# Index scores of a sparse-attention step: the high x low products on 64 rows, two heads at once

## The chip, the cores and the metric

The kernel runs on one core of a Trainium2 chip. The metric is the device time of one execution in microseconds (us); a kernel's time is the median of its runs.

## The reference

One step of a decoder layer that runs sparse attention and retention side by side, for 1024 prompt tokens and 8 sequences of 4 new tokens each. What matters here is the indexer of the sparse attention: for each query it scores every key with four small heads, and the 256 best keys are kept.

```
def index_scores(qi, wi, ki):                      # 4 heads of 64, float32
    s = jnp.einsum('bqhd,bsd->bqhs', qi, ki)
    w = wi * (N_HEADS_IDX ** -0.5 * HEAD_DIM_IDX ** -0.5)
    return jnp.einsum('bqhs,bqh->bqs', jax.nn.relu(s), w)

def select_keys(scores, q_pos, topk):
    admissible = jnp.arange(S)[None, None, :] <= q_pos[None, :, None]
    _, idx = lax.top_k(jnp.where(admissible, scores, -jnp.inf), topk)
```

Everything is float32, and the choice of keys hangs on small differences, so the scores need float32's precision.

## The kernel before, in words

**Precision.** A float32 number x is held as two FP32R numbers, high = x rounded and low = x - high, and a product is summed over high and low parts. For the projections (`terms`, lines 209 to 211) that is three products: high x high, high x low, low x high.

**Index scores.** A head has 64 numbers, half of TensorE's 128 rows. So `use_qi` (line 665) puts the query's high part into rows 0 to 63 of the tile `QS[h]` and its low part into rows 64 to 127. To do so it copies the projection's output to both halves on ACT (lines 675 and 676) and then subtracts on DVE, in place, for the low part (line 677). It is called for two heads at a time (`h0` = 0 or 2), and for two pieces of 400 tokens (`late`). `use_ki` (line 680) writes the key's high part to both halves of `KH` and its low part to both halves of `KL`. One 128-row product of `QS[h]` with `KH` is then high x high + low x high, and one with `KL` is high x low + low x low.

**The score loop** (line 705) goes over the query blocks b = 7 down to 2 of 128 tokens, each with W = 128 (b + 1) keys, and over the four heads. A head gets a buffer `pl()` in PSUM: 1024 columns, two such buffers in all. For each chunk of up to 512 keys there is a product with `KH` (line 712) and one with `KL` (line 713) into the same place. Then ACT takes the relu into `rl` (line 715, two buffers), and DVE multiplies by the head's weight and adds to `SC[b]` (lines 717 and 719).

**The order.** The program text isn't the order in which an engine issues. The kernel is built with `schedule_with_timeline_sim=True`: a planner walks the instructions with times of its own and writes down an order for each engine, and the chip keeps that order. `issue_after` puts instructions behind a given one. The helper `together` (line 169) uses it for groups of small products on parts of the array; the score loop doesn't use it. What stands in the text behind the score loop is free to run among it: the projections of the gates and of the retention (lines 209 to 211, into the two `pj` buffers), and the gather and transposes of the cached index keys for the new tokens (lines 751 to 767).

**Behind it.** The scores feed the search for the 256th largest (`pick_all`, lines 795 to 873: 32 rounds of counting, on DVE for blocks 6 to 2, on ACT for block 7 and the new tokens). The search shares the time with the retention's projections and small products; line 556 is its 64-row score product, one head on each half of the array.

Of the kernel before, what the change touches and what calls it, by code (L numbers as in the profile page):

```python
# [8 lines left out]
F32 = mybir.dt.float32  # L9
# [3 lines left out]
AF = mybir.ActivationFunctionType  # L13
OP = mybir.AluOpType
# [13 lines left out]
LK = PAST + NS  # L28
# [83 lines left out]
def hybrid_step(tc, A, outs, dbg=None):  # L112
    ctx = ExitStack()
    with ctx:
        _hybrid_step(ctx, tc, A, outs, dbg or {})


def _hybrid_step(ctx, tc, A, outs, dbg):
    nc = tc.nc
    f32 = lambda ap: ap.bitcast(F32)  # L120
# [17 lines left out]
    def pl():  # L138
        return ps.tile([128, 1024], F32, name="pl", bufs=2)

    def pt():
        return ps.tile([128, 512], F32, name="pt", bufs=2)
# [89 lines left out]
    with ExitStack() as s0:  # L232
# [127 lines left out]
        W, ws = [], []  # L360
# [288 lines left out]
    with ExitStack() as s1:  # L649
        scp = s1.enter_context(tc.tile_pool(name="scp", bufs=1, reuse_waits="tile"))  # L650
        SC = {b: scp.tile([128, (b + 1) * 128], F32, name=f"sc{b}") for b in range(2, 8)}
        SCS = scp.tile([NS, LK], F32, name="scs")
        gp = s1.enter_context(tc.tile_pool(name="gp", bufs=1, reuse_waits="tile"))
        with ExitStack() as s2:
            ip = s2.enter_context(tc.tile_pool(name="ip", bufs=1, reuse_waits="tile"))
            QS = [ip.tile([128, TT], F32R, name=f"qs{h}") for h in range(4)]
            KH = ip.tile([128, TT], F32R, name="kih")
            KL = ip.tile([128, TT], F32R, name="kil")
# [4 lines left out]
            wsc = ip.tile([128, 9, 4], F32, name="wsc")  # L663

            def use_qi(h0):
                def use(c, p):
                    sl = late[c]
                    for i in (0, 1):
                        src, q = p[64 * i:64 * i + 64], QS[h0 + i]
                        if c == 1:  # L670
                            h = 4 * (h0 + i)
                            for o in (0, 64):
                                nc.vector.tensor_copy(QF[o:o + 64, :, h:h + 4],
                                                      src[:, T - sl.start:].rearrange("p (b i) -> p b i", b=NB))
                        nc.scalar.copy(q[0:64, sl], src)
                        nc.scalar.copy(q[64:128, sl], src)
                        nc.vector.tensor_sub(q[64:128, sl], src, f32(q[64:128, sl]))
                return use

            def use_ki(c, p):  # L680
# [9 lines left out]
            for g in range(3):  # L690
                p = pt().rearrange("p (t c) -> p t c", c=128)
# [12 lines left out]

            for b in range(7, 1, -1):
                W = (b + 1) * 128
                for h in range(4):
                    p = pl()
                    for n0 in range(0, W, 512):
                        n1 = min(W, n0 + 512)  # L710
                        q = QS[h][:, b * 128:b * 128 + 128]
                        nc.tensor.matmul(p[:, n0:n1], q, KH[:, n0:n1], start=True, stop=False)
                        nc.tensor.matmul(p[:, n0:n1], q, KL[:, n0:n1], start=False, stop=True)
                    rl = ip.tile([128, LK], F32, name="rl", bufs=2)
                    nc.scalar.activation(rl[:, :W], p[:, :W], AF.Relu)
                    if h == 0:
                        nc.vector.tensor_scalar(SC[b], rl[:, :W], wsc[:, b, 0:1], None, op0=OP.mult)
                    else:
                        nc.vector.scalar_tensor_tensor(SC[b], rl[:, :W], wsc[:, b, h:h + 1], SC[b], op0=OP.mult, op1=OP.add)
                nc.vector.tensor_add(SC[b][:, W - 128:W], SC[b][:, W - 128:W], C[:, C_CAUS:C_CAUS + 128])  # L720


# [16 lines left out]
            for G in (0, 1):  # L739
                p = pt()[:, :128]  # L740
# [6 lines left out]
            for G in (0, 1):  # L747
                KP = []
                for b in range(4 * G, 4 * G + 4):
# [5 lines left out]
                    p = pt()  # L755
# [6 lines left out]
                for o in (0, 64):  # L762
                    for b4 in range(4):
                        nc.tensor.matmul(x[32 * b4:32 * b4 + 32, 8 * o:8 * o + 512], QF[o:o + 64, 4 * G + b4], KP[b4][o:o + 64],
                                         start=True, stop=True)
                for b4 in range(4):
                    nc.tensor.matmul(xn[32 * b4:32 * b4 + 32, :NS], QF[0:64, 4 * G + b4], kiT[0:64, T:], start=True, stop=True)
                rl = ip.tile([128, LK], F32, name="rl", bufs=2)
# [620 lines left out]
```

## Time and profile before

| | |
|---|---|
| median of 3 runs | 1141.44 us (1141.26 to 1142.6) |
| profiled execution | 1139.63 us, its span 1137.8 us |
| TensorE (PE) busy | 1089.7 us, 96% of the span |
| DVE busy | 679.5 us, 60% |
| ACT busy | 471.1 us, 41% |
| granted TensorE clock | 0.995 of full speed |

In the rows of the profile a line such as L712 is a line of the kernel; PE is TensorE's products, PEld its weight loads. A group row gives the engine, the operation, the tiles written and read, the tile shape with rows x columns of the array, the count, the busy time with the mean duration in ns, and the idle time before it with what ended it. A timeline row gives the start and the length in us. Durations of products overlap, because they are pipelined: what one costs is the step to the next start. A few product records are missing in the trace.

### The profile page before, as it was taken

Reading aid. Unit: us, or ns where it says so; the run is one execution under the profiler, and the core shown is the slowest. Engines: PE = TensorE matmul, PEld = TensorE weight load, DVE = VectorE, ACT = ScalarE, POOL = GpSimd, SP = SyncE. Lnnn points to the kernel's source line nnn. Section 1 sums busy time; section 2 is a strip of 40 time slices with the busy share of each in tenths; the row PEclk is TensorE's granted clock in tenths of the full one; section 3 lists DMA queues with packets and bytes.
Section 4 is the critical chain, followed back from the end, with each engine's and each line's share of the span. In section 5 each row is a group of like instructions: output and inputs, shape, how many; then the busy total and the mean of one; then the engine's idle time right before and its main releaser. Section 6 shows DMA issues by size and latency. Waiting matters only on the chain.

```text
span 1137.8 us, 20198 instructions
## 1 busy us (share of the span) xinstructions
PE 1089.7 (96%) x7978; PEld 986.6 (87%) x7978; DVE 679.5 (60%) x1637; ACT 471.1 (41%) x910; POOL 226.2 (20%) x194
## 2 busy tenths in 40 slices
PE   6989999999989999999999999999989999999997
PEld 5779788899879999999989999777989888898886
DVE  6775369999999865943223122101357767588645
ACT  6574355654565332232233322211336666443111
POOL 0012015023310311012332212143013333100000
PEclk9999999999999999999999999999999999999999
DMA  9933334135233524422876676596899741483321
GB/s 311 229 89 94 101 113 133 41 108 153 80 91 108 151 77 131 130 61 78 275 253 211 218 222 175 187 312 225 278 267 256 197 111 31 156 269 118 116 93 56
DMA packets 157237, 179.32 MB, mean 158 GB/s; under 512 B 18821, under 2 KB 129101, under 8 KB 156054
## 3 DMA queue, kind: packets, MB, share of 16 engines
q1 hardware_dynamic: 147208, 142.31, 42.4%
q0 software_dynamic: 9856, 35.66, 9.7%
q8 instruction: 63, 1.03, 0.4%
q14 instruction: 32, 0.26, 0.1%
q10 hardware_dynamic: 78, 0.06, 0.0%
HBM read 137.23 MB, written 36.98 MB: 153 GB/s over the span
## 4 chain that ended last, share of the span: by engine, by line
PE 74%; DVE 12%; DMA 5%; ACT 4%; issue 3%; SPq 1%; DVEq 0%; ACTq 0%
PE pj L209 13%; PE pj L211 13%; PE pj L210 13%; DVE eq L795 4%; PE po L1173 3%; PE pj L1327 3%; PE pj L1326 3%; PE pj L1325 3%; PE str L1014 2%; PE tr L1156 2%; PE pj L949 2%; PE pj L950 2%; PE pj L951 2%; ACT ra L802 2%; PE sx L1042 1%
## 5 line engine op out<-in xcount | busy, mean ns | idle before, releaser
L209 PE MATMUL pj<-hh,wh 128*128 128x352 f32 (+1 forms) x1168 | 384.5, 329 | 10.8 <-ACT qs L451 4.4
L211 PE MATMUL pj<-hh,wl 128*128 128x352 f32 (+1 forms) x1168 | 378.8, 324 | 0.0
L210 PE MATMUL pj<-hl,wh 128*128 128x352 f32 (+1 forms) x1168 | 378.2, 324 | 0.0
L209 PEld LDWEIGHTS pj<-hh,wh 128*128 128x128 f32 x1168 | 220.1, 188 | 20.7 <-issue 8.1
L211 PEld LDWEIGHTS pj<-hh,wl 128*128 128x128 f32 x1168 | 219.9, 188 | 4.8 <-issue 4.1
L210 PEld LDWEIGHTS pj<-hl,wh 128*128 128x128 f32 x1168 | 220.8, 189 | 2.9 <-issue 2.5
L795 DVE TENSOR_SCALAR_CACHE_REDUCE eq<-sc,cand 128x896 bf16<-128x896 f32 (+4 forms) x155 | 135.6, 875 | 2.4
L195 ACT CAST wh<-ws 128x1024 fp32r<-128x1024 f32 (+1 forms) x65 | 61.1, 941 | 115.6 <-PE pj L210 67.7
L196 DVE TENSOR_TENSOR wl<-ws,wh 128x1024 fp32r<-128x1024 f32 (+1 forms) x48 | 51.8, 1082 | 59.3 <-ACT wh L195 59.2
L196 POOL TENSOR_TENSOR wl<-ws,wh 128x1024 fp32r<-128x1024 f32 x17 | 41.4, 2437 | 166.9 <-ACT wh L195 166.7
L1143 POOL TENSOR_SCALAR lg<-lg,st 128x1024 f32<-128x1024 f32 (+7 forms) x64 | 48.2, 759 | 121.6 <-DVE st L1142 73.2
L802 ACT ACTIVATE ra<-sc,cand 128x1024 bf16<-128x1024 f32 x31 | 35.7, 1151 | 59.7 <-DVE cand L873 58.7
L1141 ACT ACTIVATE lg<-lg,st 128x1024 f32<-128x1024 f32 (+7 forms) x64 | 49.5, 775 | 24.7 <-DVE st L1140 22.5
L1016 DVE COPY kt<-str 128x512 f32<-128x512 f32 x32 | 22.1, 690 | 61.2 <-PE str L1014 57.6
L643 ACT ACTIVATE raw<-pj 128x352 f32<-128x352 f32 x48 | 22.2, 462 | 77.7 <-PE pj L211 74.5
L1325 PE MATMUL pj<-woh,MH 128*128 128x512 f32 (+1 forms) x136 | 51.3, 377 | 0.0
L1326 PE MATMUL pj<-wol,MH 128*128 128x512 f32 (+1 forms) x136 | 51.2, 377 | 0.0
L1327 PE MATMUL pj<-woh,ML 128*128 128x512 f32 (+1 forms) x136 | 51.2, 377 | 0.0
L984 POOL DMA_INDIRECT kv<-in_cache_k,idx x32 | 31.0, 968 | 98.5 <-PE str L1014 79.8
L984 POOL DMA_INDIRECT kv<-in_cache_v,idx x32 | 31.1, 972 | 74.5 <-PE sx L1042 45.4
L1156 PE MATMUL tr<-C,lg 128*128 128x128 f32 x288 | 44.5, 276 | 1.2 <-DVE pT L1158 0.3
L1156 PEld LDWEIGHTS tr<-C,lg 128*128 128x128 f32 x288 | 33.7, 140 | 9.5 <-issue 2.4
(352 smaller groups left out, 1956.3 us busy)
## 6 DMA issues: line engine op xcount, KB each, us to landing
ws<-in_w_in SPq DMA_DIRECT2D x51, 512.0 KB
TG<-raw SPq DMA_DIRECT2D x16, 528.0 KB
rot<-in_rot SPq DMA_DIRECT2D x8, 1056.0 KB
x<-in_w_ada SPq DMA_DIRECT2D x16, 512.0 KB
u<-TG SPq DMA_DIRECT2D x8, 528.0 KB
t<-TG SPq DMA_DIRECT2D x8, 528.0 KB
x<-in_x_prompt SPq DMA_DIRECT2D x8, 512.0 KB
out<-tk SPq DMA_DIRECT2D x16, 256.0 KB
```

The lines of the kernel that those rows point to most:

```text
L195: nc.scalar.copy(wh[:, :, :n], ws[:, :, :n])
L196: (nc.vector if k == 4 or len(order) % 3 else nc.gpsimd).tensor_sub(wl[:, :, :n], ws[:, :, :n], f32(wh[:, :, :n]))
L209: nc.tensor.matmul(p, wh[:, k], HH[k][:, sl], start=(k == 0), stop=False)
L210: nc.tensor.matmul(p, wh[:, k], HL[k][:, sl], start=False, stop=False)
L211: nc.tensor.matmul(p, wl[:, k], HH[k][:, sl], start=False, stop=(k == KT - 1))
L795: nc.vector.tensor_scalar(junk[:n, :W], sc, thr[:n, j:j + 1], 0.0, op0=op, op1=OP.add, accum_out=cnt[:n, j:j + 1])
L802: nc.scalar.activation(junk[:n, :W], sc, AF.Sign, bias=thr[:n, NV + j:NV + j + 1], scale=-1.0, accum_out=cnt[:n, NV + j:NV + j + 1])
L984: nc.gpsimd.indirect_dma_start(out=t.rearrange("p s c -> p (s c)"), out_offset=None, in_=cache.rearrange("g (r s) h d -> (g r) (s h d)", s ...
L1156: nc.tensor.transpose(x[:, 128 * (j - j0):128 * (j - j0) + 128], lg[:, j % 2, 128 * (j // 2):128 * (j // 2) + 128], ident)
L1325: nc.tensor.matmul(x, MH[:, k, tk], wh[:, k], start=(k == 0), stop=False)
L1326: nc.tensor.matmul(x, MH[:, k, tk], wl[:, k], start=False, stop=False)
L1327: nc.tensor.matmul(x, ML[:, k, tk], wh[:, k], start=False, stop=(k == KT - 1))
```

## The change

For the odd head of each two, the query's high part goes to rows 64 to 127 and the low part to rows 0 to 63. Since `KH` and `KL` hold the key's parts in both halves, the product with `KH` isn't touched by that. The product with `KL` now takes only the rows with the query's high part: 64 rows, the lower half of the array for the even head and the upper half for the odd head. Low x low is no longer computed. The score loop goes over two heads at a time with both `pl` buffers: per chunk both products with `KH`, then both with `KL`. In `use_qi` the high part is copied once, and the low part is the subtraction's output on the other half.

```diff
@@ use_qi
-                        nc.scalar.copy(q[0:64, sl], src)
-                        nc.scalar.copy(q[64:128, sl], src)
-                        nc.vector.tensor_sub(q[64:128, sl], src, f32(q[64:128, sl]))
+
+                        hi, lo = q[64 * i:64 * i + 64, sl], q[64 - 64 * i:128 - 64 * i, sl]
+                        nc.scalar.copy(hi, src)
+                        nc.vector.tensor_sub(lo, src, f32(hi))
@@ the score loop
             for b in range(7, 1, -1):
                 W = (b + 1) * 128
-                for h in range(4):
-                    p = pl()
+                q = [QS[h][:, b * 128:b * 128 + 128] for h in range(4)]
+                for h0 in (0, 2):
+                    ps_ = [pl(), pl()]
                     for n0 in range(0, W, 512):
                         n1 = min(W, n0 + 512)
-                        q = QS[h][:, b * 128:b * 128 + 128]
-                        nc.tensor.matmul(p[:, n0:n1], q, KH[:, n0:n1], start=True, stop=False)
-                        nc.tensor.matmul(p[:, n0:n1], q, KL[:, n0:n1], start=False, stop=True)
-                    rl = ip.tile([128, LK], F32, name="rl", bufs=2)
-                    nc.scalar.activation(rl[:, :W], p[:, :W], AF.Relu)
...
+                        for i in (0, 1):
+                            nc.tensor.matmul(ps_[i][:, n0:n1], q[h0 + i], KH[:, n0:n1], start=True, stop=False)
+
+                        for i in (0, 1):
+                            r = slice(64 * i, 64 * i + 64)
+                            nc.tensor.matmul(ps_[i][:, n0:n1], q[h0 + i][r], KL[r, n0:n1], start=False, stop=True)
+                    for i in (0, 1):
+                        h, p = h0 + i, ps_[i]
+                        rl = ip.tile([128, LK], F32, name="rl", bufs=2)
+                        nc.scalar.activation(rl[:, :W], p[:, :W], AF.Relu)
...
```

The weighting on DVE and the causal mask stand as before, now inside the loop over the two heads.

More of the change, by code (lines that the diff above doesn't have):

```diff
@@ L706, in _hybrid_step @@
                 W = (b + 1) * 128
-                for h in range(4):
-                    p = pl()
+                q = [QS[h][:, b * 128:b * 128 + 128] for h in range(4)]
+                for h0 in (0, 2):
+                    ps_ = [pl(), pl()]
                     for n0 in range(0, W, 512):
                         n1 = min(W, n0 + 512)
-                        q = QS[h][:, b * 128:b * 128 + 128]
-                        nc.tensor.matmul(p[:, n0:n1], q, KH[:, n0:n1], start=True, stop=False)
-                        nc.tensor.matmul(p[:, n0:n1], q, KL[:, n0:n1], start=False, stop=True)
-                    rl = ip.tile([128, LK], F32, name="rl", bufs=2)
[L715 to L719, printed above, removed]
+                        for i in (0, 1):
[7 more added lines that the diff above has]
+                        nc.scalar.activation(rl[:, :W], p[:, :W], AF.Relu)
+                        if h == 0:
+                            nc.vector.tensor_scalar(SC[b], rl[:, :W], wsc[:, b, 0:1], None, op0=OP.mult)
+                        else:
+                            nc.vector.scalar_tensor_tensor(SC[b], rl[:, :W], wsc[:, b, h:h + 1], SC[b], op0=OP.mult, op1=OP.add)
                 nc.vector.tensor_add(SC[b][:, W - 128:W], SC[b][:, W - 128:W], C[:, C_CAUS:C_CAUS + 128])
```

## The prediction

> **What bounds the kernel now.** I read the head of the page, then busy time by stretch, then TensorE's timeline through the score stage.
>
> ```profile
> span 1137.8 us, 20198 instructions
> PE 1089.7 (96%) x7978; PEld 986.6 (87%) x7978; DVE 679.5 (60%) x1637; ACT 471.1 (41%) x910; POOL 226.2 (20%) x194
> PE 74%; DVE 12%; DMA 5%; ACT 4%; issue 3%; SPq 1%; DVEq 0%; ACTq 0%
> ```
> ```profile
> 73.00:130.00 57.00, 55.47 (x338) 52.17 (x339) 32.25 (x53) 29.37 (x46) 10.69 (x11) 1.00 0.34 99
> 130.00:163.00 33.00, 33.00 (x198) 24.55 (x197) 14.59 (x42) 14.08 (x24) 3.15 (x2) 1.00 0.38 119
> 163.00:410.00 247.00, 233.76 (x1664) 224.02 (x1664) 233.57 (x561) 133.21 (x235) 66.82 (x34) 0.99 0.37 106
> 410.00:700.00 290.00, 288.64 (x2206) 274.18 (x2205) 115.84 (x189) 89.98 (x171) 63.62 (x51) 1.00 0.56 171
> ```
>
> The second fence gives, per stretch, its length, then busy time of PE, weight loads, DVE, ACT and POOL. TensorE is 96% of the span and 74% of the chain. The scores run from 73 to 130 us: 55.47 of 57 us busy there, DVE and ACT near half. The stretch behind them has no idle TensorE at all. From 163 to 410 the top-k search on DVE (233.57) and TensorE (233.76) are equally full, and the search waits for the scores; behind 410 TensorE is full again. So what TensorE gains or loses between 73 and 130 goes to the end one for one: both streams behind it start that much earlier or later. The 13 us that TensorE idles beside the search could hide a loss only if the search were not late too.
>
> The scores are lines 712 and 713. Their counts, and one block as it ran:
>
> ```profile
> L712 PE MATMUL pl<-kih,qs 128*128 128x512 f32 x24 | 9.6, 401 | 1.4 <-DVE qs L677 1.4
> L712 PE MATMUL pl<-kih,qs 128*128 128x384 f32 x8 | 2.7, 336 | 0.0
> L712 PE MATMUL pl<-kih,qs 128*128 128x256 f32 x4 | 1.1, 280 | 0.0
> L712 PE MATMUL pl<-kih,qs 128*128 128x128 f32 x4 | 0.9, 222 | 0.0
> ```
> ```profile
> 105.31 0.39 PE L712 MATMUL pl<-kih,qs 128*128 128x512 f32 x1
> 105.54 0.39 PE L713 MATMUL pl<-kil,qs 128*128 128x512 f32 x1
> 105.78 0.22 PE L712 MATMUL pl<-kih,qs 128*128 128x128 f32 x1
> 105.83 0.27 PE L713 MATMUL pl<-kil,qs 128*128 128x128 f32 x1
> 105.94 0.38 PE L209 MATMUL pj<-hh,wh 128*128 128x352 f32 x1
> ...
> 106.80 0.32 PE L211 MATMUL pj<-hh,wl 128*128 128x352 f32 x1
> 106.96 0.39 PE L712 MATMUL pl<-kih,qs 128*128 128x512 f32 x1
> ...
> 109.87 0.40 PE L712 MATMUL pl<-kih,qs 128*128 128x512 f32 x1
> ```
> ```profile
> 91.75 0.34 PE L713 MATMUL pl<-kil,qs 128*128 128x384 f32 x1
> 91.92 0.60 PE L757 MATMUL pt<-C,kx 128*128 128x128 f32 x4
> ...
> 96.29 0.28 PE L712 MATMUL pl<-kih,qs 128*128 128x256 f32 x1
> 96.41 0.28 PE L713 MATMUL pl<-kil,qs 128*128 128x256 f32 x1
> ```
>
> A product's price is the step from its start to the next start, since the durations overlap: 0.23 us for 512 columns (105.31 to 105.54), 0.17 for 384 (91.75 to 91.92), 0.12 for 256 (96.29 to 96.41), and 0.16 for two of 128 (105.78 to 105.94), so 0.08. There are 40 products on line 712, and as many on 713, which stands beside it in the loop.
>
> The second thing to see is the order. Head 0 of this block ends at 105.94, head 1 starts at 106.96, and projection products stand in between although the program text has the heads in a row and the projections later. The order on TensorE thus comes from a planner that takes whatever is ready; the second score buffer came free, in its reckoning, later than the first, by more than head 0's four products.
>
> **The change, part by part.**
>
> **(a) Streaming.** Per pair of heads and chunk four 128-row products become two 128-row and two 64-row ones. If the two 64-row products stream at once, one step in four goes: 12 x 0.23 + 4 x 0.17 + 2 x 0.12 + 2 x 0.08 = 3.84 us for the 20 pair-chunks. If one runs without its partner, nothing goes: it streams as many columns on half the rows.
>
> **(b) Entering and leaving the 64-row form.** The trace has no FP32R product on 64 rows; the nearest is the retention score, line 556, 64 rows by 128 columns of weights in FP32, between the same projection products.
>
> ```profile
> 202.51 0.32 PE L209 MATMUL pj<-hh,wh 128*128 128x352 f32 x1
> 202.67 0.32 PE L210 MATMUL pj<-hl,wh 128*128 128x352 f32 x1
> 202.82 0.32 PE L211 MATMUL pj<-hh,wl 128*128 128x352 f32 x1
> 203.08 0.49 PE L556 MATMUL pl<-qrT,krT 64*128 64x128 f32 x4
> ```
> ```profile
> 205.53 1.28 PE L556 MATMUL pl<-qrT,krT 64*128 64x128 f32 x18
> 206.74 0.43 PE L209 MATMUL pj<-hh,wh 128*128 128x352 f32 x1
> 207.01 0.32 PE L210 MATMUL pj<-hl,wh 128*128 128x352 f32 x1
> ```
> ```profile
> L556 PE MATMUL pl<-qrT,krT x128: 272/272/373, 196.3 to 506.5; 64*128 64x128 f32 x128
> 85.10 1.03 PE L757 MATMUL pt<-C,kx 128*128 128x128 f32 x8
> ```
>
> Four 64-row products fit in 0.49 us, where one alone takes 0.27 to 0.37, so the halves do run at once. But the way in costs: the step is 0.26 instead of 0.16 (0.10 lost), and the first 64-row product lasts 373 ns instead of 272, its weight load being uncovered (0.10). The way out: the last 64-row product starts at 205.53 + 1.28 - 0.27 = 206.54, a 128-column FP32 product takes (1.03 - 0.27) / 7 = 0.11, yet the next starts 0.20 later (0.09 lost), and its step is 0.27 instead of 0.16 (0.11). In and out together: 0.40 us. Bounds: 0, if FP32R halves didn't drain the array, up to 0.40; I take 0.40, as this is the same shape, the same neighbours and the only row there is.
>
> The Trainium skill, TensorEngine Tiling (Array Packing), section Key Properties, says that changing the tiling mode drains TensorE; it has no price, and the trace agrees with 0.40. The Trainium skill, TensorE: Matmul & The Clock Gate, Part 3, has the span of a packed pair as one product plus about 4 ns, with no term for the change of mode; by that alone the sum would be the 3.84 us gain of (a) less 0.08.
>
> With all 20 pairs kept together: 20 x 0.40 - 3.84 = +4.2 us. Even an intact pair loses, since a 512-column step saves 0.23.
>
> **(c) Do the pairs stay together?** The new text asks, per chunk: high product of head 0, of head 1, then the two 64-row ones. Head 1's first product needs the second score buffer. By the order above that buffer is ready only after head 0's four products and some projections. Then the planner has head 0's own 64-row product ready, next in the text, and issues it alone; likewise for the second chunk; head 1 follows by itself. That is in, out, in, out per head: 40 entries instead of 20, and no saving. Only the first pair of the first block has both buffers free at once, so its two pair-chunks should be intact: 2 x (0.40 - 0.23) = +0.34. The other 36: 36 x 0.40 = +14.4. Ends: +4.2 (all intact) and 40 x 0.40 = +16.0 (none).
>
> **(d) Buffers.** A pair fills both score buffers and only then are they read. ACT reads head 0 at once, and the buffer is wanted again much later:
>
> ```profile
> 106.14 0.70 ACT L715 ACTIVATE rl<-pl 128x640 f32<-128x640 f32 x1 [1.60 <-PE pl L713]
> ```
>
> Read by 106.84, next written at 109.87: 3 us of projections cover it, so I price it at nothing. Without them it would be ACT's 0.7 us per pair, up to 8 us over 12 pairs, which no row suggests.
>
> **(e) Query bits.** One of two copies per head and half goes; the subtraction stays, with its output on the other half.
>
> ```profile
> L675 ACT CAST qs<-pj 64x400 fp32r<-64x400 f32 x4 | 2.0, 490 | 2.8 <-DVE qs L677 2.6
> L676 ACT CAST qs<-pj 64x400 fp32r<-64x400 f32 x4 | 1.9, 487 | 0.0
> L677 DVE TENSOR_TENSOR qs<-pj,qs 64x400 fp32r<-64x400 f32 x4 | 2.3, 573 | 1.2 <-ACT qs L676 1.1
> PE pl L712 <- DVE qs L677: 1.4, 2, 1.0
> PE pj L209 <- DVE qs L677: 1.1, 1, 1.1
> L730 DVE TENSOR_SCALAR ptab<-ptab 128x8 int32<-128x8 int32 x1 | 0.2, 172 | 2.4 <-DMA sx<-in_sxc 2.4
> ```
>
> Eight copies of 0.49 leave ACT (these four and four like them from the other buffer). TensorE waits for the subtraction 1.1 us once, where it stands behind two copies: one copy less gives 0.5. The 1.4 stays mostly: there DVE had stood 2.4 us behind a load (line 730), and a faster ACT doesn't bring that. Bounds 0 to 1.0; I take -0.5.
>
> **Sum:** 14.4 + 0.34 - 0.5 = +14.2 us. The profiled execution took 1139.63 us, so 1153.9; the median of the runs, 1141.44, is 1.8 above it: 1155.6 us.
>
> **Rivals.**
> - **Pairs intact.** The planner reckons both buffers free within one high product. Against it: the projections between heads 0 and 1. +4.2 - 0.5 = +3.7: 1145.1 us.
> - **Half intact.** Head 1's buffer comes free during head 0's first chunk, so second chunks pair up. First pair 0.34; seven further two-chunk pairs with three entries each, 8.4, less 0.23 + 2 x (0.17 + 0.12 + 0.08) = 0.97; four one-chunk pairs alone, 8 x 0.40 = 3.2; sum 11.0 - 0.5: 1151.9 us.
> - **The array doesn't drain for FP32R halves, and pairs hold** (faster). The place is each change between lines 712 and 713; it decides once an entry with its exit costs under 3.84 / 20 = 0.19 us. For it: the two halves of line 556 do run at once. Against it: 0.40 before and behind. -3.84 - 0.5 = -4.3: 1137.1 us. The packed-span rule above gives 1137.2.
> - **No drain but no pairs**: the change doesn't do what it says, and only ACT's 0.5 us is left: 1140.9 us.
>
> **Chances.** Alone 0.55, half intact 0.15, intact 0.17, no drain with pairs 0.08, neither 0.05. A measurement here tells 0.2% (2.3 us) from no change: faster is under 1139.2, slower over 1143.7. A re-planned order may shift each case by 2 us, so a little of "intact" counts as same: faster 0.10, same 0.09, slower 0.81. The range runs from 1143 (intact, 2 us lucky) to 1159 (none intact, +16.0, and 1.5 for a wait on a buffer); it leaves out the no-drain cases.
>
> **What the profile after would show.** (a, b) 64-row products start 0.26 us or more behind the 128-row one, last some 0.1 us longer than the second of a kind, and a longer first product follows. (c) Most 64-row products stand alone between products of their own head; if pairs start within 0.01 us of each other, the intact rival holds. (e) One copy per head and half at 0.49 us, and the 1.1 us wait halved. The stretch that held 57 us should be some 14 longer, and the search should start that much later. The prediction is wrong if the 64-row step is 0.23 us with no gap around it, if pairs are kept, or if the stretch behind 163 us gives the loss back.

## The result, and the profile after

The change makes the kernel slower. The median after is 1154.89 us (1153.29 to 1158.75, 6 runs) beside 1141.35 (1139.43 to 1142.6, 6 runs) for the kernel before on the same chip. The ratio over all these runs is 1.0126, interval 1.0107 to 1.0146, so 14.4 us more, between 12.2 and 16.7; the two medians by themselves are 13.5 apart. The forecast was 1155.6, 14.2 more. Below, a difference in us is the ratio times the time of before. The profiled execution after took 1157.46 us, 2.6 over its median; compare its stages, not its total.

The head of the page after:

```profile
span 1155.7 us, 20186 instructions
PE 1108.5 (96%) x7977; PEld 991.3 (86%) x7978; DVE 678.6 (59%) x1637; ACT 467.3 (40%) x902; POOL 226.6 (20%) x194
PE 75%; DVE 11%; DMA 6%; ACT 4%; issue 3%; SPq 1%; DVEq 0%; ACTq 0%
```

TensorE has 18.8 us more busy time for the same number of products. The eight copies are gone (ACT 910 to 902 instructions). Busy time by stretch, in the columns of before:

```profile
73.00:130.00 57.00, 57.00 (x278) 42.42 (x279) 26.69 (x44) 24.23 (x36) 12.11 (x9) 1.00 0.34 100
130.00:145.00 15.00, 15.00 (x91) 11.71 (x90) 5.59 (x9) 4.73 (x10) 0.00 (x0) 1.00 0.18 55
163.00:425.00 262.00, 247.21 (x1696) 236.84 (x1694) 241.12 (x583) 137.84 (x242) 68.97 (x36) 0.98 0.38 111
425.00:715.00 290.00, 288.49 (x2226) 273.66 (x2225) 116.58 (x191) 91.15 (x174) 63.35 (x50) 1.00 0.55 169
```

In the stretch from 73 to 130 us TensorE now has no idle time at all, yet it gets through 278 products where it did 338, and through 279 weight loads where it did 339. The engine is fuller and does less: a product takes longer on average. The scores need until 142 instead of 129. All rows of the two product lines, after (the second is the 64-row one) and line 713 of before, give duration as min/median/max, then the first and last start:

```profile
L714 PE MATMUL pl<-kih,qs x40: 326/396/506, 72.0 to 141.6; 128*128 128x512 f32 x24, 128*128 128x384 f32 x8, 128*128 128x256 f32 x4, 128*128 128x128 f32 x4
L718 PE MATMUL pl<-kil,qs x40: 323/492/502, 73.3 to 141.9; 64*128 64x512 f32 x24, 64*128 64x384 f32 x8, 64*128 64x256 f32 x4, 64*128 64x128 f32 x4
```
```profile
L713 PE MATMUL pl<-kil,qs x40: 273/389/397, 73.2 to 129.3; 128*128 128x512 f32 x24, 128*128 128x384 f32 x8, 128*128 128x256 f32 x4, 128*128 128x128 f32 x4
```

The median 64-row product lasts 492 ns, the 128-row one before 389: half the rows, 0.10 us longer. Step (b) called that an uncovered weight load, and the trace agrees: the weight load of a 64-row product starts together with it (both at 123.27 in the last stretch below), that of the 128-row product ahead of it starts 0.15 us early (122.80 for 122.95). The timeline shows the order, first the first pair, then a typical later block:

```profile
73.78 0.73 PE L714 MATMUL pl<-kih,qs 128*128 128x512 f32 x2
74.44 0.49 PE L718 MATMUL pl<-kil,qs 64*128 64x512 f32 x2
74.94 0.40 PE L209 MATMUL pj<-hh,wh 128*128 128x352 f32 x1
...
111.11 0.40 PE L714 MATMUL pl<-kih,qs 128*128 128x512 f32 x1
111.44 0.49 PE L718 MATMUL pl<-kil,qs 64*128 64x512 f32 x1
111.86 0.33 PE L714 MATMUL pl<-kih,qs 128*128 128x128 f32 x1
112.12 0.32 PE L718 MATMUL pl<-kil,qs 64*128 64x128 f32 x1
...
122.95 0.39 PE L714 MATMUL pl<-kih,qs 128*128 128x512 f32 x1
123.27 0.49 PE L718 MATMUL pl<-kil,qs 64*128 64x512 f32 x1
123.69 0.43 PE L210 MATMUL pj<-hl,wh 128*128 128x352 f32 x1
123.96 0.32 PE L211 MATMUL pj<-hh,wl 128*128 128x352 f32 x1
```

"x2" at 74.44 is a pair: two 64-row products in the time of one. Only the two pair-chunks of the first pair look so. All others are "x1", each between products of its own head: 36 alone, as step (c) had it. A lone one costs a step of 0.32 on the way in (122.95 to 123.27, before 0.23), 0.42 to the next product (123.27 to 123.69, before 0.23), and that product's own step is 0.27 (123.69 to 123.96, a projection's usual step is 0.16).

The search, before and after:

```profile
L795 DVE TENSOR_SCALAR_CACHE_REDUCE eq<-sc,cand x155: 591/879/1148, 157.3 to 381.1; 128x896 bf16<-128x896 f32 x31, 128x768 bf16<-128x768 f32 x31, 128x640 bf16<-128x640 f32 x31, 128x512 bf16<-128x512 f32 x31
```
```profile
L802 DVE TENSOR_SCALAR_CACHE_REDUCE eq<-sc,cand x155: 592/879/1148, 168.9 to 398.6; 128x896 bf16<-128x896 f32 x31, 128x768 bf16<-128x768 f32 x31, 128x640 bf16<-128x640 f32 x31, 128x512 bf16<-128x512 f32 x31
```

It starts 11.6 us later and ends 17.5 later: the scores' delay is passed on, and the search itself takes 5.9 us longer. Experiments 1 and 6 are about that second part.

### The profile page after: what moved, and what is told of

It is laid out like the page before. It is cut to its first block, busy times and chain, and to the rows that moved or that the text cites. A ratio compares the mean times of both kernels' runs of the same rounds, so it can differ in the third digit from the quotient of the medians.

```text
span 1155.7 us, 20186 instructions
## 1 busy us (share of the span) xinstructions
PE 1108.5 (96%) x7977; PEld 991.3 (86%) x7978; DVE 678.6 (59%) x1637; ACT 467.3 (40%) x902; POOL 226.6 (20%) x194
## 4 chain that ended last, share of the span: by engine, by line
PE 75%; DVE 11%; DMA 6%; ACT 4%; issue 3%; SPq 1%; DVEq 0%; ACTq 0%
PE pj L209 13%; PE pj L210 13%; PE pj L211 13%; DVE eq L802 3%; PE po L1180 3%; PE pj L1334 3%; PE pj L1333 3%; PE pj L1332 3%; PE str L1021 2%; PE tr L1163 2%; ACT ra L809 2%; PE pj L956 2%; PE lg L1141 2%; PE pj L957 2%; PE pj L958 2%
## 5 line engine op out<-in xcount | busy, mean ns | idle before, releaser
L196 DVE TENSOR_TENSOR wl<-ws,wh 128x1024 fp32r<-128x1024 f32 (+1 forms) x48 | 54.8, 1143 | 61.9 <-ACT wh L195 61.8
L809 ACT ACTIVATE ra<-sc,cand 128x1024 bf16<-128x1024 f32 x31 | 35.7, 1150 | 62.5 <-DVE cand L880 61.4
```

The lines of the kernel that those rows point to most:

```text
L196: (nc.vector if k == 4 or len(order) % 3 else nc.gpsimd).tensor_sub(wl[:, :, :n], ws[:, :, :n], f32(wh[:, :, :n]))
L809: nc.scalar.activation(junk[:n, :W], sc, AF.Sign, bias=thr[:n, NV + j:NV + j + 1], scale=-1.0, accum_out=cnt[:n, NV + j:NV + j + 1])
```

## The experiments

The first four were timed beside one set of runs of the kernel before (1138.67 us), the last three beside another (1137.91). "The stage" below is the time from the first score product to the product behind the last: 56.6 us before, 70.2 after.

**1. The query bits alone.** The change of `use_qi` with the old score loop; all products on 128 rows.

```diff
 (from the kernel before)
-                        nc.scalar.copy(q[0:64, sl], src)
-                        nc.scalar.copy(q[64:128, sl], src)
-                        nc.vector.tensor_sub(q[64:128, sl], src, f32(q[64:128, sl]))
+                        hi, lo = q[64 * i:64 * i + 64, sl], q[64 - 64 * i:128 - 64 * i, sl]
+                        nc.scalar.copy(hi, src)
+                        nc.vector.tensor_sub(lo, src, f32(hi))
```

> Only the query bits of the change: odd heads' halves exchanged, one copy on ACT less per head and half; score loop as before, all products on 128 rows. Theory (the loss is the array's change between 128-row and 64-row products): no 64-row product, so no loss; 0.5 us less than before, 1140.9 us (1140.4 to 1141.4). Rival (the exchange or the copy that is gone hurts, by a re-planned order): 1144 us or more.

Measured: 1140.79 us, ratio 1.0020 (1.0010 to 1.0031), so 2.3 us slower where 0.5 faster was expected. A miss, with the wrong sign. The stage is 56.8 us, as before; the loss is in the search, which runs from 155.3 to 384.8 us, 5.7 longer than before. TensorE's longest waits there, before and in this kernel, as total, times, longest:

```profile
PE pj L209 <- ACT qs L451: 4.4, 2, 2.2
PE pt L484 <- ACT tmp L499: 3.1, 2, 2.1
```
```profile
PE pt L484 <- ACT tmp L499: 6.4, 2, 4.0
PE pj L209 <- ACT qs L451: 3.1, 2, 2.8
```

And the stretches of the search whose granted clock is lowest, first before, then in this kernel (the clock is the third column from the end):

```profile
290.00:302.00 12.00, 9.88 (x55) 9.47 (x54) 11.61 (x24) 7.68 (x14) 2.96 (x2) 0.86 0.43 135
```
```profile
230.00:242.00 12.00, 9.21 (x48) 8.92 (x47) 11.93 (x35) 4.70 (x10) 2.12 (x1) 0.86 0.56 165
290.00:306.00 16.00, 11.99 (x62) 11.68 (x61) 15.26 (x32) 7.75 (x15) 6.81 (x4) 0.79 0.33 102
```

With eight instructions fewer the planner wrote another order: 8 more projection products lie among the scores, and later ones stand differently. Two waits of TensorE in the search grew to 2.8 and 4.0 us, and at each the clock drops to half. At half clock, a mean of 0.86 over 12 us is 3.4 us, and 0.79 over 16 us is 6.7 us: 10.1 us in all beside 3.4 before, where half of the difference, 3.4 us, is lost work. The Trainium skill, TensorE: Matmul & The Clock Gate, Part 1, knows full and half clock only, decided in windows of 3413 ns; these stretches of 3.4 and twice 3.4 us agree. Over all timed runs the mean granted clock was 0.9946 before and 0.9926 here. That would be 2.3 us (0.0020 x 1139), if all of the lost clock lay on the path that ends last; the end of the next part says how far the runs bear this out.

**2. The new loop, all products on 128 rows.** After, with the exchange and the loop over two heads, but no 64-row form. Low x low is computed again.

```diff
 (from the kernel after)
-                            nc.tensor.matmul(ps_[i][:, n0:n1], q[h0 + i][r], KL[r, n0:n1], start=False, stop=True)
+                            nc.tensor.matmul(ps_[i][:, n0:n1], q[h0 + i], KL[:, n0:n1], start=False, stop=True)
```

> The changed kernel with one thing taken back: the products with KL run on all 128 rows (low x low is computed again); the loop over two heads, both buffers and the exchanged bits stay. Theory (change of form costs 0.40 us per entry and exit, 38 of them): all of the loss goes, 1140.9 us, between 1139 and 1143. Rival (taking both score buffers for a pair makes TensorE wait or the planner's order worse): some 1150 us or more stays.

Measured: 1141.69 us, ratio 1.0018 (1.0003 to 1.0034), and the stage is 56.8 us. The same line as it ran here:

```profile
L718 PE MATMUL pl<-kil,qs x40: 274/390/397, 73.8 to 129.2; 128*128 128x512 f32 x24, 128*128 128x384 f32 x8, 128*128 128x256 f32 x4, 128*128 128x128 f32 x4
```
```profile
L209 PE MATMUL pj<-hh,wh 128*128 128x352 f32 x76 | 24.8, 326 | 0.1
```

The median is back from 492 to 390 ns and the last start from 141.9 to 129.2 (the second fence is a group of the projections within the stage; it is wanted below). The 64-row form and nothing else costs the 13.4 us of the stage (70.2 - 56.8): all products of the stage stand in the same order in both kernels. The loop over two heads costs nothing, and the 2 us left are those of experiment 1. Per entry: 13.4 = 38 x price - 2 x 0.23 for the two intact pairs, so 0.365 us on average.

Since the order is the same, the steps can be set side by side. This is the lone chunk of the last stretch above, here on 128 rows:

```profile
113.18 0.39 PE L714 MATMUL pl<-kih,qs 128*128 128x512 f32 x1
113.41 0.40 PE L718 MATMUL pl<-kil,qs 128*128 128x512 f32 x1
113.64 0.32 PE L210 MATMUL pj<-hl,wh 128*128 128x352 f32 x1
113.80 0.32 PE L211 MATMUL pj<-hh,wl 128*128 128x352 f32 x1
```

With 64 rows the way in is 0.09 longer (0.32 for 0.23), the way out 0.19 (0.42 for 0.23) and the step behind 0.11 (0.27 for 0.16): 0.39 us, and nearly the same at most of the entries. The average is lower because a few are cheaper: 0.29 for each of the four short chunks of 128 columns, less where no projection follows, and no way out to speak of behind the first pair of heads, where TensorE had to wait for its next work in experiment 2 too.

**3. Pairs held together.** After, with the two 64-row products of each chunk put behind the second 128-row one.

```diff
 (from the kernel after)
-                            nc.tensor.matmul(ps_[i][:, n0:n1], q[h0 + i], KH[:, n0:n1], start=True, stop=False)
+                            high = nc.tensor.matmul(ps_[i][:, n0:n1], q[h0 + i], KH[:, n0:n1], start=True, stop=False)
...
-                        for i in (0, 1):
-                            r = slice(64 * i, 64 * i + 64)
...
+                        with tc.issue_after(high.ins):
+                            for i in (0, 1):
+                                r = slice(64 * i, 64 * i + 64)
...
```

> The changed kernel with the two 64-row products of a chunk put behind the second 128-row product, so that all 20 pairs stand together. Theory (0.40 us per entry and exit, 20 of them, less 3.84 us of streaming): before + 4.2 - 0.5 = 1145.1 us. Rival (a pair that runs at once pays for its entry; the changed kernel only lost since the pairs were apart): at or under before, 1137 to 1141 us. Rival (waiting for the second buffer costs as much as it saves): 1150 us or more.

Measured: 1152.02 us, ratio 1.0116 (1.0102 to 1.0131). A miss: 13.2 us slower than before where 3.7 was expected. The time lies where the second rival put it (1150 or more, by a wait for the second buffer); what fills that wait is told below. All 20 pairs are intact, as this stretch of the timeline shows:

```profile
107.14 0.39 PE L714 MATMUL pl<-kih,qs 128*128 128x512 f32 x1
107.37 0.32 PE L210 MATMUL pj<-hl,wh 128*128 128x352 f32 x1
107.69 0.33 PE L209 MATMUL pj<-hh,wh 128*128 128x352 f32 x1
107.86 0.39 PE L714 MATMUL pl<-kih,qs 128*128 128x512 f32 x1
108.18 0.50 PE L719 MATMUL pl<-kil,qs 64*128 64x512 f32 x2
108.61 0.50 PE L714 MATMUL pl<-kih,qs 128*128 128x256 f32 x2
```

But between head 0's product (107.14) and head 1's (107.86) there stand projections: the planner fills the wait for the second buffer. In the whole stage they are 17 more of line 209 than in experiment 2:

```profile
L209 PE MATMUL pj<-hh,wh 128*128 128x352 f32 x93 | 30.7, 330 | 0.0
```

With lines 210 and 211 it is 277 projection products in a stage of 68.2 us, 226 in experiment 2's 56.8. The 51 more at 0.16 us are 8.2 of the 11.4 us by which the stage grew. The remaining 3.3 are the array: 20 x price - 3.84 gives 0.357 per entry. So the price of an entry stood, and holding the pairs cost more than they saved: the search starts only at 167.5 us, and experiment 5 shows that the projections done early come back only in part.

**4. One entry for a pair of heads.** All 128-row products of both chunks and both heads, then all 64-row ones: 12 entries instead of 38.

```diff
 (from the kernel after)
+                            high = nc.tensor.matmul(ps_[i][:, n0:n1], q[h0 + i], KH[:, n0:n1], start=True, stop=False)
...
+                    with tc.issue_after(high.ins):
+                        for n0 in range(0, W, 512):
+                            n1 = min(W, n0 + 512)
+                            for i in (0, 1):
+                                r = slice(64 * i, 64 * i + 64)
...
```

> As the one before, but both chunks' 128-row products of the two heads first and then all their 64-row products: 12 entries into the 64-row form instead of 20. Theory: 12 x 0.40 - 3.84 = +1.0, less 0.5 for the copies: 1141.9 us, the same as before within what can be told. If the price is one per 64-row product, not per entry, it equals the kernel before it (1145). If entries are dearer than 0.40, above 1143.

Measured: 1148.21 us, ratio 1.0085 (1.0068 to 1.0103): 9.7 us slower than before where 0.5 was expected, a miss, though the products ran as meant. The second pair of heads of block 7, with two chunks of 512 columns:

```profile
80.53 0.71 PE L714 MATMUL pl<-kih,qs 128*128 128x512 f32 x2
81.18 0.73 PE L721 MATMUL pl<-kil,qs 64*128 64x512 f32 x4
81.84 0.43 PE L209 MATMUL pj<-hh,wh 128*128 128x352 f32 x1
82.11 0.32 PE L210 MATMUL pj<-hl,wh 128*128 128x352 f32 x1
```

From the first of these four 64-row products to the product behind them it is 0.66 us (81.18 to 81.84); for one pair it was 0.43 in experiment 3 (108.18 to 108.61). The second pair adds 0.23, the step of one product of 512 columns: the price is one of the passage, not of the products. Within the form the second pair isn't free of it (the trace starts it 0.33 us behind the first, not 0.23), but the way out is shorter by as much. So this group pays 0.40 and saves 2 x 0.23, a few hundredths of a us to the good. Still the stage is 64.5 us, 7.7 longer than in experiment 2, with 271 projection products in it. The mark of 1143 us, above which entries were to be dearer than 0.40, was passed for another reason.

**5. The same order on 128 rows.** Experiment 4 without the 64-row form, low x low computed again: what does the holding cost by itself?

```diff
 (from experiment 4)
-                                nc.tensor.matmul(ps_[i][:, n0:n1], q[h0 + i][r], KL[r, n0:n1], start=False, stop=True)
+                                nc.tensor.matmul(ps_[i][:, n0:n1], q[h0 + i], KL[:, n0:n1], start=False, stop=True)
```

> The kernel with one entry per pair of heads (e4), its products in the same order, but the KL products on all 128 rows: no 64-row product is left. Theory (holding both heads together lets 45 more projection products, 7.2 us, into the score stage and starts the search that much later; the array's part was 0.5 us): 1147.7 us against 1138.7 of before, as slow as e4 within 1 us. Rival (e4 lost by the 64-row products): as the kernel with all rows (e2), 1140.7 us.

Measured: 1145.53 us, ratio 1.0066 (1.0053 to 1.0079). By the ratio that is 7.5 us over before, 2.2 under experiment 4; the theory said as slow within 1 us, 9.0 over before, the rival 2.0. So most of the loss is the holding, as the theory had it, and the bound of 1 us was too narrow. The projections within its stage of 64.1 us:

```profile
L209 PE MATMUL pj<-hh,wh 128*128 128x352 f32 x91 | 29.5, 324 | 0.1
```

91 here, 76 in experiment 2; with the other two lines 45 more, and 45 x 0.16 = 7.2 is the whole growth of the stage (64.1 - 56.8). Of it 5.5 us (1.0066 against 1.0018) is in the time. Experiment 4's stage is only 0.4 us longer: 12 entries less the 3.84 saved, 0.35 us per entry. That its time is 2.2 us longer isn't clear of noise, since the intervals overlap.

**6. Both copies kept.** Experiment 1 with a second copy on ACT, which the subtraction overwrites: the exchange stays, the removal goes.

```diff
 (from experiment 1)
                         nc.scalar.copy(hi, src)
+                        nc.scalar.copy(lo, src)
                         nc.vector.tensor_sub(lo, src, f32(hi))
```

> The query bits exchanged as in e1, but ACT still makes a second copy (into the low half, which the subtraction then overwrites), so ACT has the work of before. Theory (the copy that is gone changes the planned order, and with it the waits and the halved clock in the search): the order of before comes back, 1138.7 us. Rival (the exchange of the halves itself costs): 1140.8 us, as e1.

Measured: 1138.58 us, ratio 1.0005 (0.9996 to 1.0014). As expected, the kernel before; TensorE's order is that of before instruction for instruction (one record is missing in the trace), and its longest waits in the search are nearly the same:

```profile
PE pt L484 <- ACT tmp L499: 2.8, 2, 2.2
```

The mean granted clock of its timed runs is 0.9947 (before 0.9952). So it is the removal of the copies, not the exchange of the bits, that goes with the 2 us, and the order that the planner makes of it is what differs in the search. (The intervals of experiments 1 and 6 overlap a little, so the times alone wouldn't show it.) One execution, the profiled one, had a clock of 0.991 and took 1142.33, 3.8 over the median, in the same order: its three waits of 2.2 us in the search were each followed by half clock, while in the profile of before only one of three such waits was. So it isn't the length of the wait alone that decides.

**7. The 64-row form in half of the blocks.** After, with 64 rows in blocks 6, 4 and 2 only, 20 entries, all alone.

```diff
 (from the kernel after)
-                            r = slice(64 * i, 64 * i + 64)
+                            r = slice(64 * i, 64 * i + 64) if b % 2 == 0 else slice(0, 128)
```

> The changed kernel with 64-row products in the blocks 6, 4 and 2 only; the blocks 7, 5 and 3 take all 128 rows. 20 of the 64-row products are left, each alone. Theory (0.36 us per entry, as the score stages of the kernels so far give): 1140.7 of the kernel without 64-row products (e2) + 20 x 0.36 = 1147.9 us, and a score stage of 56.8 + 7.2 = 64.0 us. Rival (the loss hangs on something that comes once, not per entry): as the changed kernel, 1152 or more, or as e2, 1141.

Measured: 1146.32 us, ratio 1.0083 (1.0064 to 1.0101); the stage 63.9 us, 7.1 over experiment 2: 0.354 us per entry. With 0, 20 and 38 entries the ratio less 1 is 0.18, 0.83 and 1.26%: the loss grows with the entries.

## Why the prediction was right, step by step

- **What bounds it** held. The stage's loss goes to the end: 13.4 us of 64-row form in the stage and some 2 of order, against 14.4 measured (12.2 to 16.7). "One for one" held within the noise for the share of the 64-row form (12.3 us of time between experiment 2 and this kernel); for work that the planner moves into the stage it doesn't quite, as 7.2 us of stage became 5.5 in experiment 5.
- **(a) Streaming** held: pairs run at once, a pair saves one step of 0.23, and what remains of experiments 3 and 4 beside the projections, 3.3 and 0.4 us, fits with 3.84 saved.
- **(b) The passage** held: 0.40 us was taken from line 556, and a lone entry between full-sized products costs 0.39 (experiment 2). Taken for all 38 it is too much, for the mean is 0.35 to 0.365 in four kernels: a short second chunk, for one, costs 0.29, which fits with a 128-column product that had its weight load half uncovered before already (273 ns at the least before, 323 after). 38 x 0.035 is 1.3 us too much. The drain that the Trainium skill, TensorEngine Tiling (Array Packing), Key Properties, states without a price fits with this; the 0.39 us hold the uncovered weight loads too, and no run separates the two. The rival that had no price for the change of form, and would have been faster, fell.
- **(c) Pairs fall apart** held exactly: 36 alone, the two chunks of the first pair whole. This was the step that chose between the cases, and it came from one order in the old timeline: projections between head 0 and head 1. That the second buffer is the reason fits with experiment 3, where projections stand in the same place; no run tried it by itself.
- **(d) Buffers at nothing** held for the change as it ran, since lone heads don't hold them. It was wrong inside the rival "intact", which was put at 3.7 us over before (1145.1): with pairs kept, experiment 3 was 13.2 over it, 2.3 of them those of (e). The "up to 8 us over 12 pairs, which no row suggests" is near what the holding costs, not as ACT's reading but as projections taken in front of the scores.
- **(e) Query bits** was wrong: -0.5 predicted, +2.3 measured (experiment 1). The local part happened, and was larger than said, as the 1.4 us that were to stay mostly went too: TensorE's waits for the subtraction in the score stage went from 2.5 us to

```profile
PE pl L714 <- DVE qs L678: 0.5, 1, 0.5
```

But the stage of experiment 1 got no shorter, as 8 more projections (1.3 us) stand in it, and the search got longer. The text allowed 2 us for a re-planned order only as an uncertainty around its cases and put none into the sum. In the search of the changed kernel the waits and the clock are those of experiment 1 (two stretches, 3.5 and 6.9 us at half clock):

```profile
PE pt L484 <- ACT tmp L499: 6.1, 2, 3.8
PE pj L209 <- ACT qs L451: 3.1, 2, 2.8
```
```profile
240.00:256.00 16.00, 13.21 (x73) 12.93 (x72) 15.75 (x44) 8.09 (x16) 2.12 (x1) 0.89 0.47 133
305.00:320.00 15.00, 11.22 (x56) 10.91 (x56) 14.29 (x31) 8.28 (x16) 5.27 (x3) 0.77 0.33 107
```

That the forecast of 1155.6 met 1154.89 within 1 us is luck in part: two errors of opposite sign stand in it, 1.3 us too much in (b) and 2.8 too little in (e), and the measured difference itself is known only to 2 us.

Open: why the planner's order without the copies has the longer waits was not tried beyond experiment 6. That the halved clock, and not the waits themselves, makes most of the 2 us is a match of sizes, not an experiment, and the record is divided. For it: the profiled execution of experiment 6, which has the order of before and a low clock, lost 3.8 us. Against it: over the 23 runs of before beside experiment 1, with clocks from 0.991 to 0.997, a straight line gives 0.4 us per 0.001 of clock, so 0.8 us for the 0.0020, and a run at 0.991 took 1137.78, under the median. No version here beats the kernel before: a lone entry costs 0.39 us and saves nothing, one pair saves 0.23 at 512 columns, and the order that needs fewest entries costs more by holding both buffers.

## What to carry to other kernels

Price a half-array product by its passage in and out and by its neighbours: here 0.39 us for a lone one, 0.36 on average, so a pair of 512 columns that saves 0.23 loses, and two such pairs behind one entry just come out ahead (0.40 against 0.46 in experiment 4). Whether pairs stay pairs is read from the order that the scheduler already made of the same buffers; forcing them together has its own price, work taken in front that the next stage waits for. An edit that only removes instructions can still lose time through the new order, so price that as a term of the sum, and look at the longest waits of TensorE in the new order, at which its clock was halved here.

## What the runs showed of the hardware

- Going into the 64-row FP32R form and out again costs 0.35 to 0.365 us of TensorE time on average in four kernels, 0.39 at a lone entry between full-sized products. A second pair behind the same entry adds only its streaming: 0.66 us from the first start to the next product for two pairs of 512 columns, 0.43 for one.
- In the stretch from 140 to 440 us of the nine profiles, all ten waits of TensorE of 3.2 to 4.0 us were followed by 3.4 or 6.8 us at half clock (the half clock can begin up to 1.4 us before the wait ends). Of the seven waits of 2.8 us five were, but not those of experiments 5 and 7; of the thirteen waits of 2.1 to 2.4 us eight were.
